# A hybrid mLSTM / forgetting-attention layer on one core: gates product ahead of the convolutions, shorter inverse roots, one value product for two attention groups, and the output products' sums spread out

## The chip, the cores and the metric

The kernel runs on one core of a Trainium2 chip. A core has five engines that this text names as the profile does: PE does the matrix products (PEld is its loading of the stationary operand), DVE and ACT do elementwise work and are the ones that read the accumulation banks, POOL does some more elementwise work, and SP issues nearly all DMA transfers from one queue. Each engine takes its instructions in order. The metric is the device time of one execution in microseconds (us).

## The reference

One layer on x of 512 tokens x 1024, all in float32: a conditioning vector c gives nine rows (shift, scale, gate for three stages) through a 1024 x 9216 matrix; then

```
u = rms_norm(x, ffn1_norm_g) * (1 + sc1) + sh1
x = x + 0.5 * g1 * swiglu(u, ffn1_w_in, ffn1_w_out)        # 1024 -> 2 x 2816 -> 1024
u = rms_norm(x, mix_norm_g) * (1 + sc2) + sh2
z = u @ w_mix + b_mix                                      # q, k, v, o, i, f of mLSTM; q, k, v, f of attention; two gates
qk = silu(causal_conv(q, k; width 4))                      # mLSTM queries and keys
h_m = mlstm(qk, v, i, f)                                   # 4 heads, 128 x 256
y_a = sigmoid(o) * rms_norm(h_m)
y_b = forgetting_attention(rms_norm(q), rms_norm(k), v, f) # 16 heads of 64
x = x + g2 * ((sigmoid(g_a) * (y_a @ w_a) + sigmoid(g_b) * (y_b @ w_b)) @ w_out)
u = rms_norm(x, ffn2_norm_g) * (1 + sc3) + sh3
x = x + 0.5 * g3 * swiglu(u, ffn2_w_in, ffn2_w_out)
```

## The kernel before

**Products.** Each float32 operand is split into a high part and the rest (`wh` by ACT, L101; `wl` by DVE, L103), and each product is three matmuls: high by high, high by low, low by high (`mm3`, L125 to L128). Weights come through rings: three raw buffers (`raw`, L91), four of `wh` and four of `wl`; a raw buffer is free again once its `wl` is made, a `wh`/`wl` pair once its matmuls are done. PSUM has four banks tagged `g` and four tagged `t`, 512 columns each.

**Order.** The program text is not the order on the engines. A planner replays the program at build time with its own estimates of durations, and at each moment gives a free engine the ready instruction that stands first in the program; what comes out is the fixed order of each engine's queue. Instructions wrapped in `pin` (`keep_in_program_order`) keep their place to each other; `issue_after` puts one behind another.

**Inverse roots.** `rsqrt` (L136) works on a few columns: an integer first guess, then a polynomial correction, ten small DVE steps, L143 to L153; the norms ahead of it (`xnorm` L242, `chain` L710) spend two more on the mean (L246 and L247, L713 and L714).

**First norm** (`start`, L693): PE transposes fillers (L726), multiplies the first conditioning columns (L742), transposes the normalized x (L731) and starts the products (L826), in a pinned order.

**Feed-forward output** (`pair_out`, L527). The product with the 2816 x 1024 matrix is done with seven half-size products for eight (sums of weights are prepared earlier in DRAM, `ws`). A first sweep of 11 steps makes Z, X, Y, whose sums are P1, U2 and U4 (L569 to L575), two tiles of each. A second sweep of 11 steps (L609) accumulates Z, Y, X, W in eight banks; each step takes two raw loads of 512 KB, every other one also an early load (L544) for the last three steps, which are left for the end (`tail` = 3) and close one bank after the other (L638). During the second sweep x is loaded again (L621), two tiles after each of steps 3 to 6 of the program, and after steps 6 and 7 the first sweep's sums are scaled by the gate row (L597) and added onto x (L600): P1 onto one quarter each, U2 onto one, U4 onto two. In the second feed-forward each closed bank is then scaled, added and stored (L607), 512 columns at a time, the last one W of tile 1. In the first feed-forward `end` (L1315) takes over instead: it pins the closing of the banks, the norm of the first half of the tokens (`xnorm(0)`, `norm_turn` L295), the splitting of the first four blocks of w_mix (`lo1`, `lo2`, `lo3`, L1328), u of the half (L275 to L280), and 192 matmuls of 256 columns (`first(0)`, L1380), then the same for the other half of the tokens. `first` goes through k in two halves and, in each, through blocks 0 and 1, then 2 and 3.

**Gates and convolutions** (L1415). The four banks of blocks 0 to 3 go through `qk_conv` (L912: ACT reads the bank into `cz`, four DVE steps make `cy`, ACT applies silu and splits, DVE makes the rest; two buffers each of `cz` and `cy`). Then `gates` (L850): a product of 280 columns (attention group 0's values and all gates) in three chunks of weights (128 x 840, 840 and 560) and the `t` banks, and a chain of small ACT and DVE steps. Then blocks 4 to 7, each a product into a `g` bank and a `qk_conv`.

**Attention** (L1462). Sixteen heads in four groups; beside the heads of one group, the products of the next (`fox_qkv`, L1039) advance step by step: 8 steps for queries and keys (512 columns), then for groups 1 to 3 the values (256 columns, 4 steps, L1089), then steps of output gates (2, 4 and 4 gates of two steps each, L1466). Value tiles have three buffers.

## Time and profile before

| | us |
|---|---|
| median of 3 runs (1333.33 to 1336.34) | 1333.39 |
| the profiled execution | 1333.93 |
| its span, first to last instruction | 1332.2 |
| PE busy in it | 1311.0 |
| DVE busy | 966.3 |
| ACT busy | 625.0 |

A profile row gives an engine, a source line, the operation with out<-in, and a time. A matmul's shown duration is from entering the array to leaving it, and neighbours overlap: a stream's pace is read from a stretch of time and the number of matmuls in it, not from that duration. In brackets stands the idle time of the engine ahead of the row, and the instruction that ended it; in the view of waits a row is: who waited, for whom, us in total, times, the longest. The chain goes back from the last instruction through what each step waited for. The granted TensorE clock is 1.0 through the whole span.

### The profile page before, as it was taken

The numbers are of one execution on the slowest core, as the hardware profiler recorded it, in microseconds if no ns is written. First come the engines' busy times: TensorE is split into PE (matmuls) and PEld (weight loads), VectorE is DVE, ScalarE is ACT, GpSimd is POOL, SyncE is SP. The second block draws the span as 40 slices with busy tenths as digits, with TensorE's granted clock in tenths as the row PEclk, the third lists the DMA queues.
The fourth block names the chain that finished last, engine by engine and source line by source line (L and its number), as shares of the span: only waits on it lengthen the run. The fifth ranks groups of instructions, "written<-read, shape, count | busy, mean of one in ns | idle before, by whom it ended". The sixth has DMA issues, their size and how long they took to land.

```text
span 1332.2 us, 18008 instructions
## 1 busy us (share of the span) xinstructions
PE 1311.0 (98%) x6428; PEld 1098.2 (82%) x6428; DVE 966.3 (73%) x1776; ACT 625.0 (47%) x1038; POOL 42.4 (3%) x65
## 2 busy tenths in 40 slices
PE   7999999999999999999999999999999999999998
PEld 6788888878788888888888788778788888888886
DVE  7877777477788687887877778777477656635777
ACT  5533323365476655566666666334253223223742
POOL 1000000000010101000000000003010000000000
PEclk9999999999999999999999999999999999999999
DMA  9999978365835334534252636777529877534574
GB/s 291 276 321 312 317 269 284 113 182 182 280 112 144 108 101 133 159 101 117 65 155 52 181 97 190 217 248 234 163 71 334 282 248 265 201 105 134 172 267 149
DMA packets 205514, 254.21 MB, mean 191 GB/s; under 512 B 15008, under 2 KB 148800, under 8 KB 205424
## 3 DMA queue, kind: packets, MB, share of 16 engines
q1 hardware_dynamic: 205040, 252.98, 60.6%
q8 instruction: 51, 0.84, 0.3%
q14 instruction: 39, 0.32, 0.1%
q0 software_dynamic: 320, 0.06, 0.0%
q10 hardware_dynamic: 64, 0.02, 0.0%
HBM read 217.28 MB, written 35.72 MB: 190 GB/s over the span
## 4 chain that ended last, share of the span: by engine, by line
PE 85%; DVE 7%; DMA 3%; ACT 3%; issue 1%; POOL 0%; ACTq 0%; SPq 0%; DVEq 0%; POOLq 0%
PE g L128 22%; PE g L127 22%; PE g L126 22%; PE t L127 3%; PE t L128 3%; PE t L126 3%; PE g L826 2%; DVE wl L103 2%; PE t L1200 1%; PE t L1170 1%; DMA raw<-in_ffn_w_out_dram 1%; ACT wh L101 1%; PE t L1141 1%; PE t L826 1%; PE t L1142 1%
## 5 line engine op out<-in xcount | busy, mean ns | idle before, releaser
L101 ACT ACTIVATE wh<-raw 128x1024 fp32r<-128x1024 f32 (+2 forms) x250 | 253.8, 1018 | 379.2 <-PE g L127 115.0
L103 DVE TENSOR_TENSOR wl<-raw,wh 128x1024 fp32r<-128x1024 f32 (+2 forms) x250 | 293.4, 1175 | 186.9 <-ACT wh L101 155.6
L127 PE MATMUL g<-ul,wh 128*128 128x512 f32 (+1 forms) x912 | 348.1, 383 | 0.6 <-DVE ul L267 0.3
L126 PE MATMUL g<-uh,wh 128*128 128x512 f32 (+1 forms) x912 | 348.2, 384 | 0.2 <-ACT wh L101 0.2
L128 PE MATMUL g<-uh,wl 128*128 128x512 f32 (+1 forms) x912 | 347.8, 382 | 0.0
L127 PEld LDWEIGHTS g<-ul,wh 128*128 128x128 f32 x912 | 171.3, 188 | 34.0 <-POOL ul L267 1.1
L128 PEld LDWEIGHTS g<-uh,wl 128*128 128x128 f32 x912 | 171.3, 188 | 33.3
L126 PEld LDWEIGHTS g<-uh,wh 128*128 128x128 f32 x912 | 170.8, 188 | 33.0 <-issue 0.6
L126 PE MATMUL g<-wh,uh 128*128 128x512 f32 (+1 forms) x288 | 103.0, 358 | 0.0
L128 PE MATMUL g<-wh,ul 128*128 128x512 f32 (+1 forms) x288 | 102.2, 355 | 0.0
L127 PE MATMUL g<-wl,uh 128*128 128x512 f32 (+1 forms) x288 | 102.0, 354 | 0.0
L325 DVE SCALAR_TENSOR_TENSOR acc<-raw,ccol,acc 128x512 f32<-128x512 f32 (+1 forms) x70 | 66.7, 973 | 30.6 <-DMA raw<-in_w_ada_dram 30.4
L127 PE MATMUL t<-wl,A 128*128 128x512 f32 x176 | 69.2, 393 | 1.1 <-DVE wl L103 1.1
L126 PE MATMUL t<-wh,A 128*128 128x512 f32 x176 | 69.3, 394 | 0.0
L126 PEld LDWEIGHTS g<-wh,uh 128*128 128x128 f32 x288 | 54.3, 189 | 7.7 <-DVE tk L1047 0.5
L128 PEld LDWEIGHTS g<-wh,ul 128*128 128x128 f32 x288 | 54.3, 188 | 7.6
L127 PEld LDWEIGHTS g<-wl,uh 128*128 128x128 f32 x288 | 54.3, 189 | 7.3
L128 PE MATMUL g<-yh,wl 128*128 128x512 f32 x128 | 50.5, 394 | 1.3 <-DVE wl L103 1.3
L127 PE MATMUL g<-yl,wh 128*128 128x512 f32 x128 | 50.2, 393 | 0.0
L126 PE MATMUL g<-yh,wh 128*128 128x512 f32 x128 | 49.9, 390 | 0.0
L455 ACT ACTIVATE A<-E 128x768 fp32r<-128x768 f32 x22 | 18.6, 846 | 55.1 <-DVE E L454 51.0
L1152 ACT ACTIVATE S<-S,mn 128x128 f32<-128x128 f32 (+1 forms) x64 | 35.6, 557 | 17.9 <-DVE mn L1144 9.3
(347 smaller groups left out, 2192.3 us busy)
## 6 DMA issues: line engine op xcount, KB each, us to landing
raw<-in_ffn_w_in_dram SPq DMA_DIRECT2D x82, 512.0 KB
raw<-in_w_ada_dram SPq DMA_DIRECT2D x56, 512.0 KB
raw<-in_w_mix_dram SPq DMA_DIRECT2D x46, 512.0 KB
sa<-in_ffn_w_out_dram SPq DMA_DIRECT2D x22, 512.0 KB
sb<-in_ffn_w_out_dram SPq DMA_DIRECT2D x44, 256.0 KB
ws<-sa SPq DMA_DIRECT2D x22, 512.0 KB
ws<-sb SPq DMA_DIRECT2D x44, 256.0 KB
raw<-ws SPq DMA_DIRECT2D x44, 256.0 KB
```

The lines of the kernel that those rows point to most:

```text
L101: nc.scalar.activation(hi, src, AF.Copy)
L103: self.last_lo = nc.vector.tensor_tensor(lo, src, hi, op=SUB)
L126: pin(mm(ps, lh, rh, start=start, stop=False))
L127: pin(mm(ps, lh, rl, start=False, stop=False))
L128: self.last_mm = pin(mm(ps, ll, rh, start=False, stop=stop))
L325: nc.vector.scalar_tensor_tensor(a, r[:, s], c, a, op0=MUL, op1=ADD)
L455: nc.scalar.activation(A1[:, 0:3, :], E[:, 0:3, :], AF.Copy)
L826: pin(nc.tensor.matmul(acc_ps[b], (wl if p == 1 else wh)[:, b % 2, s], self.ul[k] if p == 2 else self.uh[k], start=k == 0 and p == 0, stop ...
L1141: nc.tensor.matmul(ps[:, :w], q[:, s], k[:, :w], start=True, stop=False)
L1142: nc.tensor.matmul(ps[:, :w], q[:, s], kl[:, :w], start=False, stop=True)
L1152: nc.scalar.activation(S[:, ws], S[:, ws], AF.Exp, scale=-1.0, bias=m, accum_out=sm[:, qb:qb + 1])
L1170: tr = lambda b, c, qb, kb: nc.tensor.transpose(b[:, c:c + P], S[:, P_OFF[qb] + kb * P:P_OFF[qb] + (kb + 1) * P], self.ident)
```

## The change

It has five parts. `rsqrt` takes eight steps where it took ten (one integer step for two, two products of quadratic factors for a chain), and the norms' mean is one step where it was two. `gates` is called ahead of the convolutions of blocks 0 to 3; for the second half of the tokens `first` goes through all of k for blocks 0 and 1 and then for 2 and 3; `lo2` and `lo3` are made in halves, the second ones after u of blocks 4 and 5. Values of attention groups 2 and 3 are one product of 512 columns beside group 1's heads (8 steps), and the output gates are dealt 2, 2 and 6. In the feed-forward output x is loaded after steps 1 to 4, each two tiles that are made there, and the scaling (`hold`) and adding (`give`) of the first sweep's sums is dealt over steps 2 to 7. In the second feed-forward the bank W of tile 1 is closed after step 7 and added at once (`add(W[1], 0, (3,))`), and its last three steps go to a new bank in two halves of 256 columns, each scaled, added and stored by itself.

```diff
 
-    def rsqrt(self, v, n, pin=lambda i: i):
+    def rsqrt(self, v, n, pin=lambda i: i, gain=1.0):
 
...
         y = sp.tile([P, n], F32, name=self.nm("rq"), tag=f"rq{n}", bufs=4)
-        t = sp.tile([P, n], F32, name=self.nm("rt"), tag=f"rt{n}", bufs=2)
+        t, q = [sp.tile([P, n], F32, name=self.nm("rt"), tag=f"rt{n}", bufs=2) for _ in range(2)]
         d = sp.tile([P, n], F32, name=self.nm("rd"), tag=f"rd{n}", bufs=2)
         V = nc.vector
-        pin(V.tensor_scalar(y.bitcast(I32), v.bitcast(I32), 1, None, op0=ALU.logical_shift_right))
-        pin(V.tensor_scalar(y.bitcast(I32), y.bitcast(I32), -1, 0x5F3759DF, op0=MUL, op1=ADD))
+        s = (gain * RSQ_LEAD) ** 0.25
+        (a0, b0), (a1, b1) = [(a * s, b * s * s) for a, b in RSQ_QUADS]
+        pin(V.tensor_scalar(y.bitcast(I32), v.bitcast(I32), -0.5, 0x5F3759DF, op0=MUL, op1=ADD))
 
         pin(V.tensor_tensor(t, y, y, op=MUL))
-        pin(V.tensor_tensor(t, t, v, op=MUL))
-        pin(V.tensor_scalar(d, t, -1.0, 1.0, op0=MUL, op1=ADD))
-        pin(V.tensor_scalar(t, d, RSQ[0], RSQ[1], op0=MUL, op1=ADD))
-        pin(V.tensor_tensor(t, t, d, op=MUL))
-        pin(V.scalar_tensor_tensor(t, t, RSQ[2], d, op0=ADD, op1=MUL))
-        pin(V.scalar_tensor_tensor(t, t, RSQ[3], d, op0=ADD, op1=MUL))
-        pin(V.scalar_tensor_tensor(y, t, RSQ[4], y, op0=ADD, op1=MUL))
+        pin(V.scalar_tensor_tensor(d, t, -s, v, op0=MUL, op1=MUL))
+        pin(V.tensor_scalar(d, d, s, None, op0=ADD))
+        pin(V.scalar_tensor_tensor(t, d, a0, d, op0=ADD, op1=MUL))
+        pin(V.scalar_tensor_tensor(q, d, a1, d, op0=ADD, op1=MUL))
+        pin(V.scalar_tensor_tensor(y, t, b0, y, op0=ADD, op1=MUL))
+        pin(V.scalar_tensor_tensor(y, q, b1, y, op0=ADD, op1=MUL))
         return y
...
         s2 = self.ss[:, 2 * hf:2 * hf + 2, :]
-        self.pin(nc.vector.tensor_scalar(v, s2[:, :, 0], 1.0 / D, EPS, op0=MUL, op1=ADD))
-        self.pin(nc.vector.scalar_tensor_tensor(v, s2[:, :, 1], 1.0 / D, v, op0=MUL, op1=ADD))
-        r = self.rsqrt(v, 2, self.pin)
+        self.pin(nc.vector.scalar_tensor_tensor(v, s2[:, :, 0], D * EPS, s2[:, :, 1], op0=ADD, op1=ADD))
+        r = self.rsqrt(v, 2, self.pin, D ** 0.5)
         xn = []
...
         Z, Y = [[self.tbank() for _ in range(2)] for _ in range(2)]
-        banks = {"Z": Z, "Y": Y, "X": X, "W": W}
+        banks, tail = {"Z": Z, "Y": Y, "X": X, "W": W}, 3
         def prepare(i, d=None):
...
             return {"Z": (a(0), b(0)), "Y": (a(3), b(1)), "X": (a(2), b(2)), "W": (a(1), b(3))}
-        step = lambda n, tb, i, o: mm(banks[n], tb, *o[n], i == 0, i == NP - 1)
+        step = lambda n, tb, i, o: mm(banks[n], tb, *o[n], i == 0, i == NP - (1 if end or n != "W" or not tb else 1 + tail))
         if end:
...
             nc.sync.dma_start(self.out[0, tb * P:(tb + 1) * P, half * 512:(half + 1) * 512], self.x[tb][half])
-        tail, ds = 3, []
+        self.x, ts = [], {}
+        def hold(n, src, half):
+            ts[n] = scaled(src, half)
+        def give(n, tb, half):
+            onto(tb, half, ts[n])
+        spread = {2: ((hold, "p0", P1[0], 0), (give, "p0", 0, 0), (hold, "v0", U4[0], 1)),
+                  3: ((give, "v0", 0, 1),),
+                  4: ((give, "v0", 2, 1), (hold, "p1", P1[1], 0), (give, "p1", 1, 0)),
+                  5: ((hold, "u0", U2[0], 0), (give, "u0", 2, 0)),
+                  6: ((hold, "v1", U4[1], 1), (give, "v1", 1, 1), (give, "v1", 3, 1)),
+                  7: ((hold, "u1", U2[1], 0), (give, "u1", 3, 0))}
+        ds = []
         for i in range(NP - tail):
...
                     step(n, tb, i, o)
-            if i == 3:
-                self.x_tiles()
-            if 3 <= i < 7:
+            for f, *args in spread.get(i, ()):
+                f(*args)
+            if 1 <= i <= NT:
+                q = i - 1
+                self.x.append([self.xp.tile([P, 512], F32, name=self.nm("x"), tag=f"x{2 * q + h}") for h in range(2)])
                 for h in range(2):
-                    nc.sync.dma_start(self.x[i - 3][h], x_src[(i - 3) * P:(i - 2) * P, h * 512:(h + 1) * 512])
-            if i in (6, 7):
-                tb = i - 6
-                add(P1[tb], 0, (tb,))
-                add(U2[tb], 0, (tb + 2,))
-                add(U4[tb], 1, (tb, tb + 2))
+                    nc.sync.dma_start(self.x[q][h], x_src[q * P:i * P, h * 512:(h + 1) * 512])
         def close(n, tb):
...
 
+        add(W[1], 0, (3,))
         for n in "XZYW":
             for tb in range(2):
+                if n == "W" and tb:
+                    last = self.gbank()
+                    for c in (slice(0, 256), slice(256, 512)):
+                        ps, x, r = last[:, c], self.x[tb + 2][0][:, c], slice(tb * P, (tb + 1) * P)
+                        for i, o in enumerate(os):
+                            a, b = o[n]
+                            self.mm3(ps, a[0][:, r], a[1][:, r], b[0][:, c], b[1][:, c], i == 0, i == tail - 1)
+                        t = self.tmp(tp, "rs")[:, :256]
+                        nc.vector.scalar_tensor_tensor(t, ps, 0.5, g[0][:, c], op0=MUL, op1=MUL)
+                        V(x, x, t, op=ADD)
+                        nc.sync.dma_start(self.out[0, (tb + 2) * P:(tb + 3) * P, c], x)
+                    continue
                 ps = close(n, tb)
...
             s2 = self.ss[:, 2 * hf:2 * hf + 2, :]
-            pin(nc.vector.tensor_scalar(v, s2[:, :, 0], 1.0 / D, EPS, op0=MUL, op1=ADD))
-            pin(nc.vector.scalar_tensor_tensor(v, s2[:, :, 1], 1.0 / D, v, op0=MUL, op1=ADD))
-            return self.rsqrt(v, 2, pin)
+            pin(nc.vector.scalar_tensor_tensor(v, s2[:, :, 0], D * EPS, s2[:, :, 1], op0=ADD, op1=ADD))
+            return self.rsqrt(v, 2, pin, D ** 0.5)
         def norm(tb, h, dve=False):
...
             nc.vector.tensor_tensor(t3, t3, r[:, tb * 8:(tb + 1) * 8].unsqueeze(2).to_broadcast([P, 8, 64]), op=MUL)
-        bv = self.bias_bcast([(VF + o, 256)], ip) if g else None
-        vt = ip.tile([P, NT, 4, P], F32R, name=self.nm("fvt"), tag="vm", bufs=3)
+        if g == 3:
+            self.fx[g] = tok, self.fx[g]
+            return
+        gs = ((0,), (1,), (2, 3))[g]
+        n = len(gs) * 256
+        bv = self.bias_bcast([(VF + o, n)], ip) if g else None
+        vts = [ip.tile([P, NT, 4, P], F32R, name=self.nm("fvt"), tag="vm", bufs=3) for _ in gs]
         def donev(tb, ps):
-            f = ip.tile([P, 256], F32, name=self.nm("vg"), tag="t2", bufs=3)
+            f = ip.tile([P, n], F32, name=self.nm("vg"), tag="t2", bufs=3)
             if g:
-                nc.vector.tensor_tensor(f, ps[:, :256], bv[:, :256], op=ADD)
+                nc.vector.tensor_tensor(f, ps[:, :n], bv[:, :n], op=ADD)
             else:
                 nc.sync.dma_start(f, self.v0_d[tb])
-            f4 = f.rearrange("p (h d) -> p h d", h=4)
-            nc.scalar.activation(vt[:, tb, :, 0:64], f4, AF.Copy)
-            nc.vector.tensor_tensor(vt[:, tb, :, 64:P], f4, vt[:, tb, :, 0:64], op=SUB)
+            for i, vt in enumerate(vts):
+                f4 = f[:, i * 256:(i + 1) * 256].rearrange("p (h d) -> p h d", h=4)
+                nc.scalar.activation(vt[:, tb, :, 0:64], f4, AF.Copy)
+                nc.vector.tensor_tensor(vt[:, tb, :, 64:P], f4, vt[:, tb, :, 0:64], op=SUB)
         def mkv(ch):
             def make():
-                sh = [P, 4, 256]
-                r = self.raw(sh, [(lambda t: t, w[ch * 512:(ch + 1) * 512, VF + o:VF + o + 256]
+                k = 8 // (2 * len(gs))
+                sh = [P, k, n]
+                r = self.raw(sh, [(lambda t: t, w[ch * k * P:(ch + 1) * k * P, VF + o:VF + o + n]
                                    .rearrange("(k p) n -> p k n", p=P))])
                 wh, wl = self.split(r, sh)
-                return wh, wl, 4 * ch, 4
+                return wh, wl, k * ch, k
             return make
-        self.fx[g] = (tok, vt)
+        self.fx[g] = (tok, vts[0])
+        if len(gs) > 1:
+            self.fx[3] = vts[1]
         if g:
-            yield from self.u_gemm_tokens([mkv(c) for c in range(2)], 256, donev)
+            yield from self.u_gemm_tokens([mkv(c) for c in range(2 * len(gs))], n, donev)
         else:
...
                     part(2, 3)
-                    lo2()
                     u[2]()
                     u[3]()
+                    lo2(0, 4)
                     w1 = scaled(W[1], 0)
-                    lo3()
+                    lo3(0, 4)
                     part(4, 5)
...
                     onto(2, 1, tx[0, 1])
-                    onto(2, 0, tx[0, 0])
+                    lo2(4, NK)
+                    lo3(4, NK)
                     part(6, 7)
...
                     u[7]()
+                    onto(2, 0, tx[0, 0])
                     self.x_sq(2, 1, tx[0, 1])
...
                         mm = nc.tensor.matmul
-                        for ks in (range(4), range(4, NK)):
+                        for ks in ((range(NK),) if h else (range(4), range(4, NK))):
                             for ms in ((0, 1), (2, 3)):
...
         with tc.tile_pool(name="gates", bufs=1) as mp:
+            columns = self.gates(mp, yp)
             for m in range(4):
                 self.qk_conv(m, self.pp[m], yp, mp)
-            columns = self.gates(mp, yp)
             for m in range(4, 8):
...
                     g = n // 4
-                    fill = with_gates(self.fox_qkv(g + 1, ip), 4 if g else 2) if g < 3 else (s for m in range(NK) for s in self.y_a(m, yp, ip))
+                    fill = with_gates(self.fox_qkv(g + 1, ip), (2, 2, 6)[g]) if g < 3 else (s for m in range(NK) for s in self.y_a(m, yp, ip))
                 last = n >= 12
```

(`RSQ_QUADS` and `RSQ_LEAD` are the two quadratics' coefficients and their common factor.)

3 lines of the change are left out of this document (2 added, 1 removed).

## The prediction

> **What bounds the kernel now.** I read the page first, then the view of who waited for whom on PE, then the chain and the rows in time around each wait.
>
> ```profile
> span 1332.2 us, 18008 instructions
> PE 1311.0 (98%) x6428; PEld 1098.2 (82%) x6428; DVE 966.3 (73%) x1776; ACT 625.0 (47%) x1038; POOL 42.4 (3%) x65
> PE 85%; DVE 7%; DMA 3%; ACT 3%; issue 1%; POOL 0%; ACTq 0%; SPq 0%; DVEq 0%; POOLq 0%
> ```
> ```profile
> PE t L127 <- DVE wl L103: 3.9, 3, 2.8
> PE t L295 <- DVE xn L253: 0.7, 1, 0.7
> PE t L126 <- DVE hn L1027: 0.5, 1, 0.5
> ```
>
> PE is the bound: 98% busy, 85% of the chain. The time can fall in two ways only: fewer or better filled matmuls, or PE's waits taken away. All idle time of PE in the span is 1332.2 - 1311.0 = 21.2 us, a good part of it at the start and after the last matmul, so no removal of waits can give more than about 1%. The waits also say where: one of 2.8 us behind a `wl`, and the rest of those three, 1.1, in two places; the others are well under 1 us each. A change on DVE alone is worth what it takes from such a wait.
>
> **Part 1, the gates product.**
>
> ```profile
> 402.02 1.27 ACT L917 ACTIVATE cz<-g,colA 128x512 f32<-128x512 f32 x2 [4.66 <-PE g L1390]
> 403.18 2.40 ACT L101 ACTIVATE wh<-raw 128x840 fp32r<-128x840 f32 x3
> 402.82 0.55 DVE L919 TENSOR_SCALAR cy<-cz,colA 128x512 f32<-128x512 f32 x1 [4.15 <-ACT cz L917]
> 407.18 1.02 DVE L103 TENSOR_TENSOR wl<-raw,wh 128x840 fp32r<-128x840 f32 x1
> 408.26 0.40 PE L127 MATMUL t<-wl,uh 128*128 128x280 f32 x1 [2.76 <-DVE wl L103]
> ```
>
> PE stood 2.76 us at the second matmul of the gates product because DVE made its `wl` at 407.18, behind two convolutions, although ACT and DVE had been idle for over 4 us until 402. They were idle because the four `wh`/`wl` pairs are held by blocks 0 to 3 of the product before, and the first pair comes free when the third quarter of `first(1)` ends, at 402. Going through all k for blocks 0 and 1 first frees two pairs at half, near 398.7. Then `wh` (a third of 2.40 us) and `wl` (1.02) of the first chunk are done by about 401, the second by 402, while PE reaches the gates product at 404.8. The whole wait goes: 2.8 us. The third chunk needs a pair that comes free at the end of `first(1)` and is wanted 9 us later.
>
> What is late next: blocks 4 to 7 need DVE's `wl` and the `g` banks that the convolutions read. DVE has the same work after 398.5 as it had after 402.8 and starts it some 4 us earlier, PE comes 3.4 us earlier; so I put nothing down. Bounds for the part: from 0 (the wait turns up at block 4) to 2.8. The order of `first(1)` wants u of k 4 to 7 sooner. DVE had all of u done by 398.7 (402.82 - 4.15). The new order takes one k per 6 matmuls of 0.12 us (part 3) from about 392.8 on, 1.9 us of transposes after 390.89 (part 2), and wants the last of u near 398.4; u comes 0.6 us sooner by part 2, so nothing.
>
> **Part 2, inverse roots and halved splits.**
>
> ```profile
> 387.87 0.17 DVE L246 TENSOR_SCALAR v<-ss 128x2 f32<-128x2 f32 x1 [0.79 <-ACT rs L228]
> 388.07 0.16 DVE L247 SCALAR_TENSOR_TENSOR v<-ss,v 128x2 f32<-128x2 f32 x1
> ...
> 390.06 0.16 DVE L153 SCALAR_TENSOR_TENSOR rq<-rt,rq 128x2 f32<-128x2 f32 x1
> 390.26 0.88 DVE L253 TENSOR_SCALAR xn<-x,rq 128x512 f32<-128x512 f32 x2
> 390.89 0.63 PE L295 MATMUL t<-ident,xn 128*128 128x128 f32 x2 [0.72 <-DVE xn L253]
> ```
> ```profile
> 380.37 1.21 DVE L1328 TENSOR_TENSOR wl<-raw,wh 128x1024 fp32r<-128x1024 f32 x1
> 381.63 0.39 PE L1388 MATMUL g<-uh,wl 128*128 128x256 f32 x1 [0.16 <-DVE wl L1328]
> ```
>
> The twelve small steps come 0.20 us apart, (390.26 - 387.87) / 12; nine make the chain 0.60 us shorter. PE waits for this one (0.72), so 0.6 comes through. The halves of `lo2` and `lo3` take away a stop of some 0.3 us at 381.63 and a smaller one before it, but PE then only stands longer before the transposes, whose x comes off a DVE queue that is full until then: nothing more. Bounds: 0 to 1.3 (both gone).
>
> ```profile
> 11.15 1.95 PE L742 MATMUL t<-ccol,ar 128*128 128x128 f32 x16
> 12.94 0.60 PE L731 MATMUL t<-ident,xn 128*128 128x128 f32 x4
> 13.37 1.95 PE L742 MATMUL t<-ccol,ar 128*128 128x128 f32 x16
> 15.16 0.38 PE L731 MATMUL t<-ident,xn 128*128 128x128 f32 x2
> ```
> ```profile
> 970.00 0.40 PE L128 MATMUL g<-wh,ml 128*128 128x512 f32 x1
> 970.52 0.57 PE L295 MATMUL t<-ident,xn 128*128 128x128 f32 x3
> ```
>
> At the start the shorter chains give nothing: PE works without a gap from its fillers through L742, and ACT waits for that product, not for the root; if this cover went, at most two steps' 0.4 us would be in play. Before the second feed-forward the transposes at 970.52 start late by 0.3 us (the matmul before them entered at 970.00 and takes the array for 0.23, part 3); the root there is two steps shorter after the last sum, 0.4, so 0.3 comes through there, and I add 0.1 for the second half. Bounds 0 to 0.8. The roots in attention and mLSTM lie beside PE's products: nothing; at best the 0.5 that PE waited for `hn` in mLSTM.
>
> **Part 3, the values of groups 2 and 3.**
>
> ```profile
> L126 PE MATMUL g<-wh,uh 128*128 128x256 f32 x96 | 27.6, 288 | 0.0
> 1010.00:1210.00 200.00, 200.00 (x884) 165.41 (x883) 117.02 (x152) 59.77 (x68) 0.00 (x0) 1.00 0.67 226
> 396.06:404.06 8.00, 8.00 (x69) 8.00 (x68) 3.63 (x8) 3.34 (x7) 0.00 (x0) 1.00 0.01 2
> ```
>
> The 96 are three groups' values in one of the three kinds of matmul; two groups are 64, in three kinds 192. They become 96 of 512 columns. The pace: 200 us / 884 = 0.226 us for 512 columns; for 256 columns (8.00 + 0.28) / 69 = 0.120 us, where 0.28 us is a matmul's stay that the stretch cuts into. So 96 x (2 x 0.120 - 0.226) = 1.3 us; I take 1.2, since both paces come from other stages than this one. The steps beside the heads stay 20 for each of the two groups (8 + 8 + 4, and 8 + 12), and the weights split per matmul stay the same; DVE gets four 512-column sums for eight of 256. Bounds 0 to 1.3. The Trainium skill, TensorE: Matmul & The Clock Gate, section Back-to-back issue gap, gives an isolated gap of N/2.4 + 2.5 ns; by it the two halves cost only 2.5 ns more than the whole, an estimate of 0.24 us for the part and 1328.6 for the time. The trace does not follow it: 0.120 and 0.226 stand against its 0.109 and 0.216.
>
> **Part 4, the last tile.**
>
> ```profile
> 1327.43 0.69 DVE L597 SCALAR_TENSOR_TENSOR rs<-g,gb 128x512 f32<-128x512 f32 x1 [0.62 <-PE g L128]
> 1328.15 0.69 DVE L600 TENSOR_TENSOR x<-x,rs 128x512 f32<-128x512 f32 x1
> 1329.40:1330.60 1.20, 0.00 (x0) 0.00 (x0) 0.00 (x0) 0.00 (x0) 0.00 (x0) 1.00 0.58 219
> L863 DVE TENSOR_TENSOR v<-t,bb 128x256 f32<-128x256 f32 x4 | 1.7, 420 | 0.4 <-DMA v_d<-v 0.3
> ```
>
> After PE's last matmul stand two DVE steps of 0.69 and a store whose 256 KB move in about 1 us (219 GB/s over 1.2 us). With 256 columns the steps take 0.42, 0.54 us less together; the store is half, 0.5 less if its rows of 1 KB move at the same rate, nothing if each costs as much as one of 2 KB. PE pays 18 x 0.120 - 9 x 0.226 = 0.1 more, and DVE still has the tile before when the first half closes, 0.1. So 0.8, bounds 0.3 to 1.0. Adding the first eight steps of W at the start of the end costs two DVE steps where DVE waits for PE anyway.
>
> **Part 5, sums over six steps.**
>
> ```profile
> 1288.44 0.86 SPq L621 DMA_DIRECT2D x<-x_d  x2
> 1294.69 0.69 DVE L600 TENSOR_TENSOR x<-x,rs 128x512 f32<-128x512 f32 x1 [0.53 <-DMA x<-x_d]
> 1282.00:1298.00 16.00, 16.00 (x72) 13.27 (x71) 13.15 (x16) 6.67 (x7) 0.00 (x0) 1.00 0.92 339
> 1289.39 8.21 DMA raw<-in_ffn_w_out_dram
> 1298.80 1.24 DVE wl L103
> 1300.08 0.50 PE L127 MATMUL t<-wl,A 128*128 128x512 f32 x1 [0.76 <-DVE wl L103]
> ```
>
> The wait at 1300 is about 1 us (the chain's steps come one after the other: raw load 8.21, ACT, `wl`, PE). The planner had already pulled the loads of x to the moment when their buffers come free, the end of steps 1 to 4 of the second sweep, and the adds with them; the program text now only says so. What made the wait is a load of 512 KB that took 8.21 us while the DMA engines were 0.92 busy, and the bytes don't change. What changes is which sum waits for which x and that SP issues x ahead of the next raw loads. I take 0.5 for both sweeps together. Bounds: a gain of 1.5 (the 1.1 of the view of waits, and two restarts of 0.2) to a loss of 6.2: if an add for x of token tile 2, queued on DVE as its program place allows, stands ahead of two splits until x lands 6.25 us after its issue, as in the rows above, the splits come 3.1 us late, in each sweep.
>
> **Sum.** 2.8 + 0.6 + 0.4 + 1.2 + 0.8 + 0.5 = 6.3 us off the profiled execution's own 1333.93 (0.54 above the median shown): 1327.6.
>
> **Rivals.** (a) The gates' wait only moves: DVE makes the `wl` of blocks 4 and 5 late, behind the convolutions. For it: DVE is the engine that PE waited for, and convolutions held a `wl` for over 4 us (402.82 to 407.18). Against: the lead of 4 us that it gets. Without part 1: 1330.4, no difference that can be told. (b) Slower: the banks.
>
> ```profile
> 420.41 0.48 PE L126 MATMUL g<-uh,wh 128*128 128x512 f32 x1
> 433.19 0.63 ACT L896 ACTIVATE ggm<-gfs 4x512 f32<-4x512 f32 x1 [1.95 <-DVE gfs L895]
> ```
>
> Block 4's product takes a `g` bank that a convolution has read. If the planner puts the first `cz` behind the gates' chain, as the program text now has it, block 4, due 3.4 us earlier than before at 417.0, waits for the chain's last ACT step, which would end near 430.4, and for one `cz`, 0.6: some 14 us, 1341.6. From a wait of 6.3 us on the change is slower. Against it: `cz` is ready long before the gates' sums are, and the planner takes what is ready. (c) The adds on DVE hold the splits up, part 5's loss: 1327.6 + 0.5 + 6.2 = 1334.3, no difference. (d) The merged values run no faster than the narrow ones: 1328.8. The Trainium skill's gap formula, cited in part 3, points this way.
>
> **Chances.** A measurement of this kernel can tell 0.3%, 4 us, from no change: faster is below 1329.4, slower above 1337.4. The forecast 0.56, (d) 0.10: faster 0.66. (a) 0.15, (c) 0.07: same 0.22. (b) 0.12: slower. The range goes from all upper bounds together (2.8 + 1.3 + 0.8 + 0.5 + 1.3 + 1.0 + 1.5 = 9.2, 1324.7) to (a) with parts 2 and 5 at nothing and part 4 at its lower bound (1333.93 - 1.2 - 0.3 = 1332.4); it leaves out (b) and (c), 0.19.
>
> **What the profile after would show.** Part 1: no PE row at the gates product with an idle time over 0.3, first `wl` of 128x840 before 402. Rival (a) or (b): a PE wait at block 4 or 5, named `wl` or `cz`. Part 2: nine steps 0.20 apart, the transposes' wait of 0.72 nearly gone. Part 3: 64 matmuls of 256 columns fewer in each kind, and a PE count down by 87 (96 fewer there, 9 more in part 4). Part 4: under 4.4 us from the last matmul's end to the span's end, where 4.8 were. Part 5: the wait near 1300 at 0.5 or gone. The prediction is wrong if new waits of PE in the long middle, where the planner's order changes as a whole, sum to more than the 3 us that lie between forecast and (a).

## The result, and the profile after

The changed kernel takes 1329.49 us (median of 5 runs, 1328.02 to 1329.88). The kernel before, run beside it, takes 1334.26 us (5 runs, 1333.33 to 1336.34). The ratio is 0.996, with a 95% interval from 0.9946 to 0.9973. The forecast was 1327.6 us, with a range from 1324.7 to 1332.4. So the change is faster by 2.7 to 5.4 per thousand, as forecast in sign, and 1.9 us slower than the forecast time.

The page of the changed kernel begins with the span and the busy times:

```profile
span 1327.7 us, 17790 instructions
PE 1310.0 (99%) x6341; PEld 1092.5 (82%) x6341; DVE 961.4 (72%) x1744; ACT 622.5 (47%) x1038; POOL 43.6 (3%) x65
```

PE has 87 matmuls fewer, 6428 less 6341, as counted in the prediction. Its view of waits (the sum in us, how often, the longest one):

```profile
PE g L128 <- DVE wl L104: 1.5, 3, 0.7
PE g L128 <- POOL ul L267: 1.0, 3, 0.5
PE g L127 <- DVE rs L657: 0.8, 1, 0.8
...
PE t L295 <- DVE xn L253: 0.4, 1, 0.4
...
PE t L128 <- DVE wl L104: 0.2, 1, 0.2
```

The lines of the products have moved down by one, so `PE t L128` here answers to `PE t L127` of before. That row had 3.9 us in three waits, 2.8 of it at the gates product and the rest in the feed-forwards; now it has one wait of 0.2 us, in a feed-forward. The wait for `xn` is halved from 0.7. Two rows are new and cost time: PE waits for `wl` three times in a `g` bank (the feed-forwards), and once for a step of the last tile, L657. The 1.0 us for POOL's `ul`, in the norm ahead of the second feed-forward, is no new cost: from the output product to that feed-forward PE's waits sum to 1.0 us in both profiles.

The next table cuts both profiled spans at the start of the first matmul of each stage and takes the differences. "Second feed-forward" and "first feed-forward" here run from the first matmul on `A` to the next stage; matmuls on `A` whose weights are `we`, those of the last three steps, are not counted as matmuls on `A` in it.

| stretch | before, us | after, us | difference |
|---|---|---|---|
| start to first matmul on `A` | 267.45 | 267.76 | +0.31 |
| first feed-forward, to the first norm transposes | 106.50 | 107.24 | +0.74 |
| mixing norm, to the second group of transposes | 16.94 | 15.84 | -1.10 |
| to the last matmul of the gates product | 29.25 | 26.29 | -2.96 |
| to the first mLSTM product | 64.98 | 65.66 | +0.69 |
| mLSTM, to the first value product of attention | 105.75 | 105.66 | -0.09 |
| attention's value products | 229.48 | 228.26 | -1.21 |
| to the branch product | 16.91 | 16.91 | 0.00 |
| branch product | 90.86 | 89.46 | -1.40 |
| output product and third norm, to the first matmul on `A` | 293.05 | 292.69 | -0.36 |
| second feed-forward, to its last matmul on `A` | 101.53 | 102.07 | +0.54 |
| to the end of the span | 9.46 | 9.86 | +0.40 |

The differences sum to -4.4 us; the spans differ by 1332.16 - 1327.70 = 4.46. Three stretches went the wrong way that part 4 and part 5 touch: both feed-forwards and the end. One stretch gained that the change doesn't touch, the branch product.

At the gates product the records of ACT, DVE and PE in the changed kernel answer to those shown of before:

```profile
399.10 1.70 ACT L102 ACTIVATE wh<-raw 128x840 fp32r<-128x840 f32 x2 [1.79 <-PE g L1421]
400.03 1.98 DVE L104 TENSOR_TENSOR wl<-raw,wh 128x840 fp32r<-128x840 f32 x2 [1.48 <-ACT wh L102]
404.78 0.29 PE L127 MATMUL t<-wh,uh 128*128 128x280 f32 x1
```

Both chunks' `wl` are done at 402, and PE, there at 404.78, doesn't wait.

### The profile page after: what moved, and what is told of

It is laid out like the page before. It is cut to its first block, busy times and chain, and to the rows that moved or that the text cites. A ratio compares the mean times of both kernels' runs of the same rounds, so it can differ in the third digit from the quotient of the medians.

```text
span 1327.7 us, 17790 instructions
## 1 busy us (share of the span) xinstructions
PE 1310.0 (99%) x6341; PEld 1092.5 (82%) x6341; DVE 961.4 (72%) x1744; ACT 622.5 (47%) x1038; POOL 43.6 (3%) x65
## 4 chain that ended last, share of the span: by engine, by line
PE 87%; DVE 5%; DMA 4%; ACT 2%; issue 1%; POOL 0%; ACTq 0%; SPq 0%; DVEq 0%; POOLq 0%
PE g L129 23%; PE g L127 23%; PE g L128 23%; PE t L127 3%; PE t L128 3%; PE t L129 3%; PE g L846 2%; PE t L1229 1%; DVE wl L104 1%; PE t L1199 1%; DMA raw<-in_ffn_w_out_dram 1%; PE t L1170 1%; DMA raw<-ws 1%; PE t L846 1%; ACT wh L102 1%
## 5 line engine op out<-in xcount | busy, mean ns | idle before, releaser
L128 PE MATMUL g<-ul,wh 128*128 128x512 f32 (+1 forms) x912 | 348.1, 383 | 1.0 <-POOL ul L267 1.0
L127 PE MATMUL g<-uh,wh 128*128 128x512 f32 (+1 forms) x912 | 348.5, 384 | 0.0
L128 PEld LDWEIGHTS g<-ul,wh 128*128 128x128 f32 x912 | 171.2, 188 | 34.2 <-POOL ul L267 1.8
L127 PEld LDWEIGHTS g<-uh,wh 128*128 128x128 f32 x912 | 171.0, 188 | 32.9 <-issue 0.6
L127 PE MATMUL g<-wh,uh 128*128 128x512 f32 (+1 forms) x256 | 97.4, 380 | 0.0
L129 PE MATMUL g<-wh,ul 128*128 128x512 f32 (+1 forms) x256 | 96.6, 377 | 0.0
L128 PE MATMUL g<-wl,uh 128*128 128x512 f32 (+1 forms) x256 | 96.4, 377 | 0.0
L128 PE MATMUL t<-wl,A 128*128 128x512 f32 x176 | 69.2, 393 | 0.2 <-DVE wl L104 0.2
L127 PE MATMUL t<-wh,A 128*128 128x512 f32 x176 | 69.2, 393 | 0.0
L129 PEld LDWEIGHTS g<-wh,ul 128*128 128x128 f32 x256 | 48.2, 188 | 9.0
L127 PEld LDWEIGHTS g<-wh,uh 128*128 128x128 f32 x256 | 48.2, 188 | 8.7 <-DVE tk L1067 0.5
L128 PEld LDWEIGHTS g<-wl,uh 128*128 128x128 f32 x256 | 48.2, 188 | 8.4
L127 PE MATMUL g<-yh,wh 128*128 128x512 f32 x128 | 50.4, 394 | 0.0
L128 PE MATMUL g<-yl,wh 128*128 128x512 f32 x128 | 49.7, 389 | 0.0
L128 PE MATMUL g<-wl,A 128*128 128x512 f32 x108 | 42.8, 396 | 1.5 <-DVE wl L104 1.5
```

What stands on the lines that cost most here:

```text
L127: pin(mm(ps, lh, rh, start=start, stop=False))
L128: pin(mm(ps, lh, rl, start=False, stop=False))
L129: self.last_mm = pin(mm(ps, ll, rh, start=False, stop=stop))
```

## The experiments

All medians, each with its ratio to the kernel before that ran beside it (1335.79 us for `a_no_spread`, `a_two_banks`, `best` and `b_parts123`, 1335.05 for `after_again`, `a_old_adds`, `b_gates` and `b_values`, 1334.47 for the other four; between these three groups the ratios compare, not the times):

| run | edit | us | ratio, 95% interval |
|---|---|---|---|
| after_again | the changed kernel | 1329.15 | 0.9960, 0.9947 to 0.9972 |
| a_no_spread | without part 5 | 1327.94 | 0.9946, 0.9934 to 0.9959 |
| a_two_banks | last halves in two banks | 1328.19 | 0.9948, 0.9935 to 0.9962 |
| best | both of these | 1326.61 | 0.9937, 0.9924 to 0.9949 |
| b_parts123 | before, parts 1 to 3 | 1328.36 | 0.9944, 0.9932 to 0.9956 |
| a_old_adds | new loads of x, old adds | 1329.85 | 0.9965, 0.9953 to 0.9978 |
| a_x_pool | x on GpSimd's queue | 1333.35 | 0.9989, 0.9979 to 0.9998 |
| b_gates | before, part 1 | 1330.79 | 0.9968, 0.9958 to 0.9979 |
| b_gates_call | before, the call's place alone | 1330.23 | 0.9967, 0.9954 to 0.9980 |
| b_values | before, part 3 | 1333.38 | 0.9989, 0.9980 to 0.9998 |
| b_lo | before, halves of part 2 | 1334.98 | 1.0001, 0.9992 to 1.0011 |
| best_x_pool | best, x on GpSimd's queue | 1334.82 | 1.0003, 0.9994 to 1.0013 |

The intervals are as wide as many of the effects, so the traces decide, and the times only confirm.

### The last tile: two halves in one bank

```diff
-                    last = self.gbank()
                     for c in (slice(0, 256), slice(256, 512)):
-                        ps, x, r = last[:, c], ...
+                        ps, x, r = self.gbank()[:, c], ...
```

> The changed kernel with one edit: each half of the last tile gets a bank of PSUM of its own. Theory: the first matmul of the second half waits for DVE's read of the first half (0.94 us at 1322.35 in the changed kernel's trace) only because both halves lie in one bank. Then that wait goes, 0.9 to 1.0 us of PE time comes through to the end, and the time is 1328.5 us. Rival: the wait is for DVE itself or for the array's own change of tile, and stays; or the last store queues behind the first half's and gives the gain back; then 1329.5 us.

The records of PE and of DVE at the last tile in the changed kernel:

```profile
1321.30 0.28 PE L129 MATMUL g<-we,Ra 128*128 128x256 f32 x1
1322.35 0.39 PE L127 MATMUL g<-we,A 128*128 128x256 f32 x1 [0.78 <-DVE rs L657]
...
1321.27 0.69 DVE L600 TENSOR_TENSOR x<-x,rs 128x512 f32<-128x512 f32 x1
1321.88 0.42 DVE L657 SCALAR_TENSOR_TENSOR rs<-g,gb 128x256 f32<-128x256 f32 x1
```

And PE's with two banks:

```profile
1319.93 0.28 PE L129 MATMUL g<-we,Ra 128*128 128x256 f32 x1
1320.05 0.28 PE L127 MATMUL g<-we,A 128*128 128x256 f32 x1
```

In one bank the first matmul of the second half starts 1.05 us after the one before it, where 0.12 is the pace. It waits for DVE to read the first half, and DVE comes late to that because it still adds the tile before (1321.27). With two banks the next matmul comes 0.12 us later. From the last matmul on `A` to the end of the span it is 9.46 us before, 9.86 in the changed kernel, 8.82 with two banks (and 8.82 in `best`), and 9.52 without parts 4 and 5. The rival fell; the whole 1.03 us came through. The Trainium skill, PSUM — Partial Sum Buffer, section PSUM bank collisions raise a hardware error, says that two engines must not touch the same 32 partitions of one bank at the same time, even in different columns of it, and that the guard should therefore go by bank. This trace agrees: the halves share no column, and the second still waits 0.78 us for the read of the first. The two halves are also parts of one tile of the program, so the run doesn't tell a guard by bank from a guard by tile; a bank for each half removes both.

### The sums over six steps

```diff
-            for f, *args in spread.get(i, ()):
-                f(*args)
-            if 1 <= i <= NT:
...
+            if i == 3:
+                self.x_tiles()
+            if 3 <= i < 7:
+                for h in range(2):
+                    nc.sync.dma_start(self.x[i - 3][h], ...)
+            if i in (6, 7):
+                tb = i - 6
+                add(P1[tb], 0, (tb,))
+                add(U2[tb], 0, (tb + 2,))
+                add(U4[tb], 1, (tb, tb + 2))
```

> The changed kernel with part 5 alone undone (x loaded in one run from step 3 on, the sums put onto it in steps 6 and 7). Theory: the adds spread over six steps made the new waits that the trace of the changed kernel has in both feed-forwards (0.84 + 0.37 + 0.12 us near 1286 to 1298, 0.33 + 0.82 us near 340 to 352), against 1.03 and 0.51 us in the kernel before. Then one wait per feed-forward near 361 and 1295, of about 0.5 and 1.0 us, comes back, the others go, and the kernel is 1.3 us faster than the changed one, 1328.2 us. Rival: the waits come from weight loads that share the DMA engines with x whichever way x is loaded, and fall where they like; then the time stays within 0.4 us of the changed kernel's 1329.5. Forecast of the prediction: 0.5 us slower than the changed kernel, 1330.0.

Then the changed kernel unaltered, for a second profile:

> The changed kernel once more, unaltered, beside the others of this call. It tells which waits belong to the kernel and which to the single run. If the waits on a weight load's split are the kernel's, PE's waits in the two feed-forwards' second sweeps sum again to about 2.9 us (2.4 us in the changed kernel with two banks), against 1.2 to 1.9 us in the four traces with the old adds; the branch stage (837 to 928 us before), where the five traces of the change's variants hold from 0 to 2.0 us of such waits, is expected to differ again by up to 1 us from the changed kernel's own 0.48 us, and the gain of 1.4 us there is then the run's and not the change's. Time: 0.996 of the kernel before, as measured.

And the changed kernel with its loads of x and the old adds:

```diff
-            for f, *args in spread.get(i, ()):
-                f(*args)
             if 1 <= i <= NT:
...
+            if i in (6, 7):
+                tb = i - 6
+                add(P1[tb], 0, (tb,))
+                add(U2[tb], 0, (tb + 2,))
+                add(U4[tb], 1, (tb, tb + 2))
```

> The changed kernel with half of part 5 undone: x is loaded tile by tile at the end of steps 1 to 4 as in the changed kernel, the sums go onto it in steps 6 and 7 as before. Theory: an add that waits on DVE for x stands ahead of a split, the split frees the raw buffer late, and the next weight load is issued late; so with the adds back in steps 6 and 7 the waits of 0.84 + 0.37 + 0.12 us (second feed-forward) and 0.33 + 0.82 us (first) fall to the 0.2 to 1.0 us per feed-forward of the old form, and the time is about 1 us below the changed kernel's. Rival: x's loads, ahead of weight loads on SP's queue, are the cause; then the waits stay at 2.4 to 2.9 us in both feed-forwards together.

PE's waits in the second sweeps of both feed-forwards, from the records of the changed kernel:

```profile
340.07 0.50 PE L128 MATMUL g<-wl,A 128*128 128x512 f32 x1 [0.16 <-DVE wl L104]
352.17 0.50 PE L128 MATMUL g<-wl,A 128*128 128x512 f32 x1 [0.65 <-DVE wl L104]
...
1286.30 0.50 PE L128 MATMUL g<-wl,A 128*128 128x512 f32 x1 [0.67 <-DVE wl L104]
1294.98 0.50 PE L128 MATMUL t<-wl,A 128*128 128x512 f32 x1 [0.21 <-DVE wl L104]
```

Of the kernel without part 5:

```profile
361.14 0.50 PE L128 MATMUL t<-wl,A 128*128 128x512 f32 x1 [0.34 <-DVE wl L104]
...
1293.07 0.50 PE L128 MATMUL t<-wl,A 128*128 128x512 f32 x1 [0.63 <-DVE wl L104]
```

And with the new loads and the old adds:

```profile
340.54 0.50 PE L128 MATMUL g<-wl,A 128*128 128x512 f32 x1 [0.42 <-DVE wl L104]
352.49 0.50 PE L128 MATMUL g<-wl,A 128*128 128x512 f32 x1 [0.49 <-DVE wl L104]
363.08 0.50 PE L128 MATMUL t<-wl,A 128*128 128x512 f32 x1 [0.52 <-DVE wl L104]
...
1296.61 0.50 PE L128 MATMUL t<-wl,A 128*128 128x512 f32 x1 [0.38 <-DVE wl L104]
```

Summed over such rows, eight traces with x's loads at the old place on SP's queue have 0.8 to 1.4 us of waits: before 1.10, without part 5 0.97, `best` 1.00, parts 1 to 3 0.79, `b_gates` 1.44, `b_values` 1.36, `b_lo` 1.26, `b_gates_call` 0.76. Four traces with them at the new place have 1.2 to 2.5: 1.69, 2.46 in the second profile of the changed kernel, 1.20 with two banks, 1.81 with the old adds. The first kind waits one to three times, the second four times in each trace, and each wait delays PE by some 0.3 us more than its idle time (1286.30: the next two matmuls start 0.84 and 0.11 us later than the pace, the idle time is 0.67). So part 5 costs some 1.3 us (0.74 + 0.54 in the table of stretches), and the forecast of 0.5 gained fell. The loss is shown for the first feed-forward, whose stretch takes 106.07 to 107.10 us in the eight traces (mean 106.5) and 107.22 to 108.13 in the four (mean 107.6). In the second the stretches overlap, 101.15 to 101.83 us against 101.33 to 102.47, and two of the four are no slower than the eight, so the 0.54 there may be the run's.

The theory that the adds do it fell too, for the first feed-forward. With the adds back in steps 6 and 7 the waits near 340 and 352 stay, and the time is 1329.85. Only the wait near 1286 is gone with the old adds; whether the adds made that one is open. What the loads do is seen on SP's queue in the first feed-forward. Of the changed kernel:

```profile
329.90 1.73 SPq L634 DMA_DIRECT2D x<-in_x_dram  x2
331.73 0.38 SPq L92 DMA_DIRECT2D raw<-ws  x1
...
324.89 2.49 DVE L104 TENSOR_TENSOR wl<-raw,wh 128x1024 fp32r<-128x1024 f32 x2 [1.07 <-ACT wh L102]
...
338.79 2.49 DVE L104 TENSOR_TENSOR wl<-raw,wh 128x1024 fp32r<-128x1024 f32 x2 [1.17 <-ACT wh L102]
```

Of the kernel without part 5:

```profile
328.12 0.33 SPq L92 DMA_DIRECT2D raw<-ws  x1
331.19 0.81 SPq L621 DMA_DIRECT2D x<-in_x_dram  x2
```

The bytes are the same and x is loaded at nearly the same time. But in the changed kernel the load of x, which waits for its own buffer until 329.90, stands ahead of a weight load whose buffer DVE gave back at 327.4 (324.89 + 2.49). That weight load is issued 3.6 us later than without part 5 (331.73 against 328.12), and it lands 2.5 us later (337.6 against 335.1). PE meets it at 340: the first of the two `wl` that begin at 338.79 is made from it and ends near 340.0, and PE's matmul at 340.07 takes it.

```diff
-                    nc.sync.dma_start(self.x[q][h], x_src[q * P:i * P, ...])
+                    nc.gpsimd.dma_start(self.x[q][h], x_src[q * P:i * P, ...])
```

> The changed kernel with x loaded through GpSimd's queue in place of SP's, all else as in the changed kernel. Theory: in the changed kernel a weight load stands on SP's queue behind a load of x that waits for its buffer; in the first feed-forward the raw buffer is free when a split ends at 327.4 us, yet its load is issued at 331.73, behind x at 329.90, against 328.12 where the old x loads stand behind it. With x on another queue that wait of 3 to 4 us goes, and PE's waits in the two second sweeps fall from 2.9 to 4.0 us (two profiles of the changed kernel) to the 1.2 to 2.4 us of the old form or under it; 1.3 us faster than the changed kernel, ratio 0.995 of the kernel before. Rival: the DMA engines' share is the cause, 0.92 busy whichever queue issues; then the waits stay, 0.996.

With x on GpSimd's queue the weight load is issued at 327.70, and the waits at 340 and 352 are gone, as the theory says. The time is worse all the same, because the planner then puts another load late. Of this kernel:

```profile
1288.92 0.42 SPq L544 DMA_DIRECT2D we<-ws  x1
...
1298.02 1.06 ACT L545 ACTIVATE we<-we 128x1024 fp32r<-128x1024 f32 x1 [4.79 <-DMA we<-ws]
...
1300.08 0.49 PE L127 MATMUL g<-wh,A 128*128 128x512 f32 x1 [1.08 <-ACT wh L102]
```

`we`, the weights of the last steps, was issued at 1283.90 in the changed kernel. Here it comes 5 us later, ACT stands 4.79 us for it, and two `wh` that PE needs sooner are behind it. So the queue's order is shown as the cause of the two early waits; that the remedy on another queue would pay isn't shown, since it changed a second thing.

The fastest version of the first group of runs (below), with the same edit to its loads of x:

> The changed kernel with part 5 undone, the last tile's halves in two banks, and x loaded through GpSimd's queue: what the runs so far point to. The version with x on SP's queue ran at 0.9937 of the kernel before with 1.9 us of waits of PE in the two second sweeps. If the queue is the cause of what is left of them, up to 1 us more: 0.993. If not, 0.9937 again.

The same wait for `we` came here in both feed-forwards; 1334.82 us.

### Part 1 alone, and half of it

```diff
 # b_gates: both edits of part 1; b_gates_call: this one only
+            columns = self.gates(mp, yp)
             for m in range(4):
                 self.qk_conv(m, self.pp[m], yp, mp)
-            columns = self.gates(mp, yp)
```

> The kernel before with part 1 alone. Forecast of the prediction: 2.8 us faster than the kernel before, the wait of 2.76 us at the gates product's second matmul gone and nothing new behind it. By the changed kernel's trace 0.64 us of it is lost again up to 483 us, where the transposes of gz wait for DVE: 2.2 us faster. Rival (a): the wait only moves to block 4 or 5: no gain. Rival (b): 14 us slower. The traces without part 5 show the transposes of gz without a wait, so this kernel tells too whether the 0.64 us are part 1's.

> The kernel before with one half of part 1: the gates product is called ahead of the convolutions, the last product's order over k stays. By the prediction's mechanism the first two pairs of wh and wl come free only at 402 us; then wh (0.85 us a chunk) and wl (0.99 us) are done at 403.9 and 404.9, so that PE, there at 404.8, waits for at most 0.1 us: nearly the whole 2.8 us comes from the call's place, and the order over k was not needed. Rival: the pairs at 402 are too late, because the planner still puts a convolution's steps between them; then 1 us or more of the wait stays.

From the second group of transposes to the last matmul of the gates product it is 26.28 us with part 1 alone and 26.29 with the call's place alone, against 29.25 before. So the order over k in `first(1)` wasn't needed. With the call's place alone the first chunk comes no sooner, but nothing stands between:

```profile
402.18 1.70 ACT L101 ACTIVATE wh<-raw 128x840 fp32r<-128x840 f32 x2 [4.67 <-PE g L1390]
403.12 1.98 DVE L103 TENSOR_TENSOR wl<-raw,wh 128x840 fp32r<-128x840 f32 x2 [4.30 <-ACT wh L101]
```

The first `wl` ends near 404.1, and PE starts the product at 404.98. What comes back later, up to the first mLSTM product, is 0.7 us in `b_gates`, 0.6 of it at the transposes of `gz`, and 0.5 in `b_gates_call`. Of `b_gates`:

```profile
407.39 1.06 ACT L101 ACTIVATE wh<-raw 128x1024 fp32r<-128x1024 f32 x1 [0.88 <-DMA raw<-in_w_mix_dram]
...
419.10 0.32 PE L880 MATMUL t<-ident,gz 128*96 128x128 f32 x1 [0.17 <-DVE gz L862]
```

ACT stands 0.88 us for block 4's weights ahead of the convolutions' steps. In the four traces where it stands at most 0.32 us there, the transposes of `gz` lose 0.1 us at most; in the six where it stands 0.62 to 0.89, they lose 0.4 to 0.6. That goes together, but was not tested by itself, and `b_gates_call`, whose order there is another, stands 2.68 us without such a cost at `gz`.

### Part 3 alone

```diff
-        bv = self.bias_bcast([(VF + o, 256)], ip) if g else None
+        gs = ((0,), (1,), (2, 3))[g]
+        n = len(gs) * 256
+        bv = self.bias_bcast([(VF + o, n)], ip) if g else None
...
-                    fill = with_gates(self.fox_qkv(g + 1, ip), 4 if g else 2) if g < 3 else ...
+                    fill = with_gates(self.fox_qkv(g + 1, ip), (2, 2, 6)[g]) if g < 3 else ...
```

> The kernel before with part 3 alone (values of groups 2 and 3 in one product of 512 columns). Forecast: 1.2 us faster, all of it between the first score product (590.9 us) and the last value product (820.4 us), a stretch of 229.5 us before, 228.3 us then. Rival (d), a gap of 2.5 ns per matmul: 0.24 us faster. The planner's order in the rest of the kernel should stay as before.

The records of PE, first and last value product, before and then with part 3 alone:

```profile
590.87 0.39 PE L1200 MATMUL t<-Ph,fvt 128*128 128x512 f32 x1
...
820.35 0.28 PE L1200 MATMUL t<-Pl,fvt 128*128 128x256 f32 x1
```

```profile
593.43 0.39 PE L1209 MATMUL t<-Ph,fvt 128*128 128x512 f32 x1
...
821.66 0.28 PE L1209 MATMUL t<-Pl,fvt 128*128 128x256 f32 x1
```

The stretch goes from 229.48 to 228.23 us, 1.25 less, where 1.2 was forecast and rival (d) had 0.24. (The expectation called the stretch's start a score product; it is the first value product.)

### Part 2, the halves alone

```diff
-                    lo2()
                     u[2]()
                     u[3]()
+                    lo2(0, 4)
...
                     onto(2, 1, tx[0, 1])
-                    onto(2, 0, tx[0, 0])
+                    lo2(4, NK)
+                    lo3(4, NK)
                     part(6, 7)
...
+                    onto(2, 0, tx[0, 0])
```

> The kernel before with the second half of part 2 alone: lo2 and lo3 in halves, and one sum moved behind them. Mixing norm, from the first transposes to the last group's: 16.94 us before, 15.84 with the whole change. The prediction put 0.6 on the three steps off the chain of small steps and nothing on the halves, by which it stays 16.94 here, PE only standing longer before the transposes. Rival: the halves' own stops of 0.34 and 0.42 us (379.9 and 381.6) come through in full: 16.3 here, and the rest of the 1.1, about 0.4, is the shorter chain's.

From the first transposes to the second group it is 16.64 us, 0.30 less than before. The two stops near 380 are gone, 0.34 and 0.42 us, and PE then stands 1.18 us before the transposes in place of 0.72:

```profile
388.20 0.17 DVE L246 TENSOR_SCALAR v<-ss 128x2 f32<-128x2 f32 x1 [0.79 <-ACT rs L228]
...
391.22 1.94 PE L295 MATMUL t<-ident,xn 128*128 128x128 f32 x14 [1.18 <-DVE xn L253]
```

Both stories were half right: most of the stops only moved, but the chain starts 13.62 us after the first transposes (388.20 - 374.58), and 13.92 before. The remaining 0.80 of the 1.10 is the shorter chain. In the changed kernel:

```profile
388.62 0.16 DVE L247 SCALAR_TENSOR_TENSOR v<-ss 128x2 f32<-128x2 f32 x1 [0.79 <-ACT rs L229]
...
389.62 0.16 DVE L151 SCALAR_TENSOR_TENSOR rt<-rd 128x2 f32<-128x2 f32 x1
389.70 0.15 DVE L152 SCALAR_TENSOR_TENSOR rt<-rd 128x2 f32<-128x2 f32 x1
389.81 0.16 DVE L153 SCALAR_TENSOR_TENSOR rq<-rt,rq 128x2 f32<-128x2 f32 x1
...
390.21 0.88 DVE L253 TENSOR_SCALAR xn<-x,rq 128x512 f32<-128x512 f32 x2
```

The nine steps take 1.59 us, not 1.79: two of them don't need the step ahead of them and come 0.08 and 0.11 us behind it.

### What the runs point to

The kernel before with the diff's edits of parts 1 to 3:

> The kernel before with parts 1, 2 and 3 alone. By the traces of before and after, parts 4 and 5 together cost 1.3 us in the feed-forwards and 0.3 us at the end (1.04 us of wait and 0.1 us of narrower matmuls against 0.85 us of shorter tail), so without them the time is 1.6 us under the changed kernel's: 1327.9 us, 6.3 us under the kernel before. By the prediction's own terms (parts 4 and 5 worth 0.8 + 0.5 us) it would be 1.3 us above the changed kernel's, 1330.8 us.

The changed kernel with the edits of `a_no_spread` and `a_two_banks` together:

> The changed kernel with part 5 undone and the halves of the last tile in two banks. If both theories hold their gains add: 1.3 + 0.95, 1327.2 us. If only one holds, 1328.2 or 1328.5 us; if neither, 1329.5 us.

Parts 1 to 3 alone ran at 0.9944, below the whole change at 0.996; without parts 4 and 5 the kernel isn't slower. `best`, with part 5 undone and two banks in part 4, ran at 0.9937, 1326.61 us, and its span of 1324.8 us is 2.9 and 3.7 under the two profiles of the changed kernel. It is the fastest version here; its interval overlaps that of the changed kernel by 0.0003.

The gain of 1.40 us in the branch product is the run's. The records of PE there, of before and of parts 1 to 3:

```profile
838.75 0.50 PE L128 MATMUL g<-yh,wl 128*128 128x512 f32 x1 [0.86 <-DVE wl L103]
889.45 0.50 PE L128 MATMUL g<-yh,wl 128*128 128x512 f32 x1 [0.49 <-DVE wl L103]
```

```profile
884.48 0.50 PE L129 MATMUL g<-yh,wl 128*128 128x512 f32 x1 [1.26 <-DVE wl L104]
```

The first profile of the changed kernel has 0.22 us of such waits there, the second none. Such a wait comes and goes between profiles whose program is alike in this stage.

## Why the prediction was right, and where it was not

The direction and the range held, and rivals (a), (b) and (d) didn't come. But the time was right for reasons that are partly others. By the table, the change itself is worth 3.3 us between these two profiles, 2.96 - 0.69 + 1.10 + 0.36 + 1.21 - 0.40 - 1.28, where the prediction has 6.3. Parts 1 to 3 gave 4.9 us of it where 5.0 were forecast; parts 4 and 5 lost 1.7 where 1.3 of gain were forecast. Of the 3.0 us missing, the branch product's 1.40, which no part of the change made, covers nearly half: that the time came out only 1.9 us from the forecast is luck to this extent. By the prediction's own line for "faster", 1329.4, the median of 1329.49 lies just on the other side; the 95% interval of the ratio still lies wholly below 1.

One reading that stands ahead of the sum was wrong. Of the waits of PE that it doesn't show the prediction says "the others are well under 1 us each"; the same view of before has one of 4.8 us (the rows of `b_ada` at the start), two that sum to 2.6 and one of 0.9. No term rests on it.

- **Part 1, 2.8 forecast.** The product's wait is gone, 2.96, without a wait at the product and with the first `wl` before 402, as the signs said. "I put nothing down" for the work behind it was 0.7 too good in this trace, a small piece of rival (a), and 0 to 0.7 in the others. The measured times give part 1 more than its trace, 4.3 us, for a reason that the forecast doesn't have (a lower clock, seen behind the wait in two profiles and in the means of most runs that have the wait, last section). The mechanism was right in the convolutions, and more than needed in the pairs: the call's place alone gives the same.
- **Part 2, 1.0 forecast.** 1.10 at the mixing norm and 0.36 behind the output product (0.4 forecast there). Two terms of the sum were too small: the chain (0.6 forecast, 0.80 measured), since "nine make the chain 0.60 us shorter" gave every step 0.20 us; and the halves ("nothing more" forecast, 0.30 measured).
- **Part 3, 1.2 forecast.** 1.25 alone, 1.21 in the change. Right, by the paces from the rows. The isolated gap of the Trainium skill, TensorE: Matmul & The Clock Gate, section Back-to-back issue gap, gave 0.24, and these runs don't follow it.
- **Part 4, 0.8 forecast.** The step that failed is "PE pays 18 x 0.120 - 9 x 0.226 = 0.1 more". The tail from the last matmul's end is shorter, as forecast: with a stay of 0.28 us, 1323.41 + 0.28 to 1327.70, or 4.0 us, under the 4.4 of the sign. But the second half's first matmul waits for the read of the first half, since both lie in one bank, and PE pays about 1 us. Net 0.40 lost; with two banks 0.64 gained (9.46 to 8.82).
- **Part 5, 0.5 forecast.** The sign was wrong; 1.28 lost, inside the bounds given. The failed step is "The planner had already pulled the loads of x to the moment when their buffers come free ... the program text now only says so". The moment was within some 1.4 us of the old one, but not the place on SP's queue, and a weight load with a free buffer stood 3.6 us longer. The sentence that SP "issues x ahead of the next raw loads" named the right thing and put no price on it. The sign, the wait near 1300 "at 0.5 or gone", came true all the same, as the new waits lie elsewhere. Rival (c), adds that hold splits up, isn't the cause in the first feed-forward; the wait near 1286 is left open.

## What to carry to other kernels

When a transfer moves by one place on an in-order queue, look at what stands behind it and whether that has its buffer already: the time at which the moved transfer itself starts tells nothing of its cost. Before an output tile is split so that its first half can be drained early, give the halves banks of their own. And a single profile can't tell a gain of 1 us from a wait that comes and goes with the loads: take the same stage from several profiles before giving it a cause, and look at the granted clock of all runs, not of the profiled one alone.

## What the runs showed of the hardware

The wait that part 1 removed costs more in other executions than in the profile of before. The table of stretches of time there (busy times of PE, its weight loads, DVE, ACT and GpSimd, then the granted clock, the DMA share and GB/s), of before, of `b_values` and of `b_lo`, which all have the wait:

```profile
411.00:414.00 3.00, 3.00 (x25) 3.00 (x25) 3.00 (x6) 1.07 (x1) 0.00 (x0) 1.00 0.86 230
```

```profile
408.00:411.00 3.00, 1.71 (x11) 1.71 (x12) 3.00 (x5) 2.45 (x5) 0.10 (x1) 0.90 0.16 26
411.00:414.00 3.00, 3.00 (x15) 3.00 (x14) 3.00 (x6) 1.41 (x3) 0.00 (x0) 0.53 0.90 241
```

```profile
408.00:411.00 3.00, 2.41 (x12) 2.42 (x13) 3.00 (x5) 2.41 (x5) 0.10 (x1) 0.71 0.37 82
411.00:414.00 3.00, 3.00 (x19) 3.00 (x19) 3.00 (x6) 1.06 (x1) 0.00 (x0) 0.72 0.96 262
```

After the same wait of 2.76 us, two of three profiles show a lower clock: 3 x (0.10 + 0.47) = 1.7 us of full clock are missing in the one and 3 x (0.29 + 0.28) = 1.7 in the other. From the matmul that waited to the last one of the gates product it is 13.4 us in both, and 11.9 in the profile of before. Part 1 alone gains 4.3 us by its median (0.9968, 2.8 to 5.6 us), though its trace has 2.3 less than before up to the first mLSTM product; the 1.5 us of slow clock in some executions of the kernel before would fill most of that.

The mean granted clocks of the runs go with it, though a mean over the whole span doesn't say where the clock was low. Of 53 runs of the kernel before, timed beside the others, 31 have a mean of 0.998 or 0.997 and only 8 have 1.000, as the profile of before has; of the 22 runs of `b_values` and `b_lo`, which keep the wait, 15 are at 0.998 or 0.997. Of the 18 runs of `b_gates`, `b_gates_call` and `b_parts123`, which don't have the wait, none is below 0.999. The 27 runs of before at 0.998 have a median of 1335.1 us, the 8 at 1.000 one of 1333.7. The Trainium skill, TensorE: Matmul & The Clock Gate, section What's actually happening, has the clock halved after an idle window of about 3.4 us, in windows that run on freely. The missing 1.7 us are 3.4 us at half clock, which agrees; the wait here is shorter than such a window, which does not.

Shorter stops close together came before a low clock too, in one profile. In `best_x_pool` PE waits 0.74 and 0.95 us within 1.5 us near 364, and then:

```profile
366.00:368.00 2.00, 2.00 (x6) 1.51 (x6) 1.62 (x3) 0.14 (x1) 0.00 (x0) 0.50 1.04 296
```
